# Layer 0 of a two-layer encoder: branch B first, in Strassen pairs, then attention; part of the conditioning and of the slice sums on GpSimd

## Chip, core and metric

One core of one Trainium2 chip runs the whole program. The metric is device time in microseconds (us) of one execution. The profile calls the engines PE (TensorE), PEld (its weight loads), DVE (VectorE), ACT (ScalarE), POOL (GpSimd) and SP (SyncE, which issues the transfers).

## What is computed

Two layers on a sequence of 512 positions with 2048 channels, in float32. Both are conditioned by a vector c: shift, scale and gate are `silu(c) @ w_mod + b_mod`, 48 tiles of 128 channels per layer (16 each).

```python
# layer 0
h = rms_norm(x, g) * (1 + scale) + shift
q, k, v, z_a, u_b, g_b, g_c, z_b = split(h @ w_in)      # eight times 1024 channels
y_a = dilated_mixture_attention(rope(q), rope(k), v) * silu(z_a)   # 8 heads of 128
y_b = g_b * short_conv(g_c * u_b, conv_w) * silu(z_b)
x = x + gate * (concatenate([y_a, y_b]) @ w_out)
# layer 1: a gated unit with position mixing and three projections of 2048 channels,
# its own conditioning, then x + gate * (y @ w_out) and a last rms_norm
```

## The kernel before

**Exact products.** Every float32 weight slice and activation is split into a rounded part and a remainder (`hi`, `lo`), and a product is three matmuls (`mm3`, L336 to L341). Weights come from memory in slices of 128x1024. A `Stream` (L252) loads each slice, ScalarE casts it to `hi` (L279), VectorE subtracts to get `lo` (L280), and it runs two slices ahead of TensorE (`next`, L323).

**Plain and Strassen tiles.** `fmajor` (L354) makes one tile of 128 channels by 512 positions out of two slices: 48 matmuls of 512 columns. `paired` (L426) makes two tiles out of four slices by Strassen's scheme: seven products of 24 matmuls of 256 columns, 168 in all. It needs sums of slices (`combined`, L283: four of the seven operands need one addition each, all on VectorE) and sums of activation blocks (`Blocks.block`, L372). Before the change pairs are used in both output projections and in layer 1, not in layer 0's input projection.

**Layer 0.** A first stage forms the normalised `h`, shift and scale, and the columns of three small groups (`AB_GROUPS`, L48). Then a loop over heads (from L690) does attention and branch B together: per head the plain tiles of q and k, `u_b`, then `scores` (L628), `g_c`, then `turned` (L647: transposes of the probabilities), `z_b`, `weighed` (L657: probabilities times values) and `g_b`. Halfway it makes the second half of the values (`tmajor`, L465). The list `AB_PLAN` (L54 to L57) is the order of the slices.

**Conditioning beside it.** `Later` (L500) is called once per slice. It spreads 64 conditioning tiles (16 gates of layer 0, all 48 of layer 1) over 88 slices. Each tile is two transfers of 128x1024 and two fused multiply-and-sum instructions on VectorE (L240). GpSimd has only the rotary products (L624) in this stage.

**Order.** A program builder places each engine's instructions in a fixed order; every engine, and SP's queue of transfers, works in that order. Buffers are few: two pairs `whi`/`wlo` and three `wraw` for weight slices, two `mraw` for conditioning.

Of the kernel before, what the change touches and what calls it, by code (L numbers as in the profile page):

```python
# [14 lines left out]
D = 2048  # L15
# [22 lines left out]
def wide(c0, n):  # L38
# [12 lines left out]
    [(A_Q, P), (A_K, P), (B_Z, P), (B_GB, P)],  # L51
# [27 lines left out]

SG_PLAIN = 3  # L80
# [29 lines left out]
def trunk(ctx, tc, xT, vecs, ab_wm, sg_wm, ab_wp, ab_wg, ab_wi, ab_wo, sg_wi, sg_wo, wsT, bs, rope, band, eye, out):  # L110
# [12 lines left out]

    class Pages:


        def __init__(self):
            self.g = [work.tile([P, 4, S], F32, tag="xy", bufs=4, name="xy") for _ in range(4)]
# [91 lines left out]
    cs = const.tile([P, KT], F32, name="cs")  # L220
    nc.scalar.activation(out=cs, in_=vec[:, V_C:V_C + KT], func=AF.Tanh, scale=0.5)
    nc.vector.scalar_tensor_tensor(out=cs, in0=cs, scalar=1.0, in1=vec[:, V_C:V_C + KT], op0=ALU.add, op1=ALU.mult)
    for i in range(4):
        acc = bank()
        for j in range(4):
            kt = 4 * i + j
            nc.tensor.matmul(acc[:, j * P:(j + 1) * P], lhsT=cs[:, kt:kt + 1].to_broadcast([P, P]), rhs=ident, start=True, stop=True)
        if i % 2:
            nc.vector.tensor_copy(out=cb[:, i * S:(i + 1) * S], in_=acc)
        else:  # L230
            nc.scalar.copy(out=cb[:, i * S:(i + 1) * S], in_=acc)

    wm = {"ab": (ab_wm, V_ABB), "sg": (sg_wm, V_SGB)}

    def mod_tile(pool, n, nt, bufs):
        src, b = wm[n]
        for h in range(2):
            raw = pool.tile([P, HALF], F32, tag="mraw", bufs=bufs, name="mraw")
            nc.sync.dma_start(out=raw, in_=src[nt, h])
            nc.vector.tensor_tensor_reduce(  # L240
                out=raw, in0=raw, in1=cb[:, h * HALF:(h + 1) * HALF], scale=0.5,
                scalar=v1(b + nt) if h == 0 else macc[n][:, nt:nt + 1], op0=ALU.mult, op1=ALU.add,
                accum_out=(mods if h else macc)[n][:, nt:nt + 1])

# [7 lines left out]
    class Stream:  # L252
# [3 lines left out]
        def __init__(self, src, n, pairs=()):  # L256
# [26 lines left out]
        def combined(self, i, p):  # L283
# [3 lines left out]
            def add(a, b):  # L287
                nc.vector.tensor_tensor(out=r[a], in0=r[a], in1=r[b], op=ALU.add)  # L288
                return r[a]

            if p == 0:
                r[0] = self.load(i, self.pool, "wsum", 2)
                of = r[0]
            elif p == 1:
                r[1] = self.load(i + 1, work, "wraw", 3)
                of = add(0, 1)
            elif p == 2:
                r[2] = self.load(i + 2, work, "wraw", 3)
# [3 lines left out]
            elif p == 4:  # L302
                nc.vector.scalar_tensor_tensor(out=r[1], in0=r[1], scalar=-1.0, in1=r[2], op0=ALU.mult, op1=ALU.subtract)
                of = r[1]
            elif p == 5:
                r[3] = self.load(i + 3, work, "wraw", 3)
                of = r[3]
            else:
                of = add(0, 3)
            self.count = getattr(self, "count", 0) + 1  # L310
            return self.split(of, *((self.pool, 1) if self.count % 3 == 0 else (work, 2)))

        def ahead(self, upto):
# [50 lines left out]

    class Blocks:
# [3 lines left out]
        def __init__(self, pool, act, halves):  # L369
            self.pool, self.act, self.halves, self.sums = pool, act, halves, [None, None]  # L370

        def block(self, j, raw=None):  # L372
# [31 lines left out]
            op(u, t, a22, ALU.add)  # L404
# [3 lines left out]
            if not j:  # L408
                self.fill("wfill", 32)

        def fill(self, tag, n):

            t = self.pool.tile([P, n], F32, tag=tag, bufs=1, name=tag)
            nc.gpsimd.memset(t[:, 0:1], 0.0)
# [50 lines left out]
    def tmajor(pos, act):  # L465

        accs = [bank() for _ in range(NT)]
        for i in range(8):
            hi, lo = pos.slice()
            for k in range(2):  # L470
                kt = 2 * i + k
                cs = slice(k * S, (k + 1) * S)
                for j, acc in enumerate(accs):
                    ts = slice(j * P, (j + 1) * P)
                    a = act[kt]
                    mm3(acc, (a[0][:, ts], a[1][:, ts]), (hi[:, cs], lo[:, cs]), kt == 0, kt == KT - 1)
        return accs
# [18 lines left out]
    s_abi, s_abo = Stream(ab_wi, len(AB_PLAN)), Stream(ab_wo, len(ABO_PLAN), PAIRS_OUT)  # L496
# [3 lines left out]
    class Later:  # L500


        def __init__(self, pool, tiles, slices):
            self.pool, self.tiles, self.step, self.at = pool, tiles, len(tiles) / slices, 0.0
# [8 lines left out]
        def one(self):  # L513
            n, nt = self.tiles.pop(0)
            mod_tile(self.pool, n, nt, 2)
            if n == "sg" and KT <= nt < 2 * KT:
                mod_scale(n, nt - KT)
# [74 lines left out]
    y = Pages()  # L592
    for f in range(6):
        twice_silu(gates[f], y[f])
    fetch(1, range(KT - 4, KT))
    quarter(1, 3)
    for f in range(2):
        twice_silu(sums[1][:, f], y[6 + f])
# [14 lines left out]
    nc.sync.dma_start(out=bandT[:, :896], in_=band)  # L613

    def values(accs):
        return [split_to(acc, "v", 4, pb) for acc in accs]
# [375 lines left out]
```

## Time and profile before

| | |
|---|---|
| median of 3 runs | 1703.43 us (1702.12 to 1704.23) |
| the profiled execution | 1700.17 us, span of its instructions 1698.4 us |
| PE busy | 1635.2 us, 96% |
| DVE busy | 1237.2 us, 73% |
| ACT busy | 626.0 us, 37% |
| POOL busy | 157.9 us, 9% |
| bytes moved | 276.36 MB, mean 163 GB/s |

A busy time counts an instruction from its start to its end, waiting for a shared resource included. Matmul records overlap, so the pace of matmuls is read from their starts.

### The profile page before, as it was taken

The numbers are of one execution on the slowest core, as the hardware profiler recorded it, in microseconds if no ns is written. First come the engines' busy times: TensorE is split into PE (matmuls) and PEld (weight loads), VectorE is DVE, ScalarE is ACT, GpSimd is POOL, SyncE is SP. The second block draws the span as 40 slices with busy tenths as digits, with TensorE's granted clock in tenths as the row PEclk, the third lists the DMA queues.
The fourth block names the chain that finished last, engine by engine and source line by source line (L and its number), as shares of the span: only waits on it lengthen the run. The fifth ranks groups of instructions, "written<-read, shape, count | busy, mean of one in ns | idle before, by whom it ended". The sixth has DMA issues, their size and how long they took to land.

```text
span 1698.4 us, 23314 instructions
## 1 busy us (share of the span) xinstructions
PE 1635.2 (96%) x9294; PEld 1430.9 (84%) x9294; DVE 1237.2 (73%) x1686; ACT 626.0 (37%) x894; POOL 157.9 (9%) x110
## 2 busy tenths in 40 slices
PE   5898999999999999999999999999989999999996
PEld 4677787888888888888899988888889999988995
DVE  7899649776766777766978781224988887897874
ACT  3232324232323322323644451222244444464551
POOL 2465620000000000000000000000000000000002
PEclk7999999999999999999999999999999999999998
DMA  8787544665667665664544422222123333335322
GB/s 310 246 289 281 179 133 145 225 227 203 215 212 239 210 227 191 221 214 146 173 139 141 168 100 87 95 92 99 63 100 100 100 117 118 102 119 191 100 88 100
DMA packets 86989, 276.36 MB, mean 163 GB/s; under 512 B 8800, under 2 KB 13152, under 8 KB 86880
## 3 DMA queue, kind: packets, MB, share of 16 engines
q1 hardware_dynamic: 86880, 274.87, 47.8%
q8 instruction: 73, 1.20, 0.3%
q14 instruction: 36, 0.29, 0.0%
HBM read 266.45 MB, written 8.39 MB: 162 GB/s over the span
## 4 chain that ended last, share of the span: by engine, by line
PE 82%; DVE 10%; issue 2%; DMA 2%; ACT 2%; POOL 0%; SPq 0%; DVEq 0%; ACTq 0%; POOLq 0%
PE ps L341 27%; PE ps L340 27%; PE ps L339 27%; DVE mraw L240 3%; DVE wlo L280 2%; DMA mraw<-in_ab_wm_dram 1%; PE ps L856 1%; ACT whi L279 1%; PE ps L653 1%; DMA wraw<-in_ab_wp_dram 1%; DVE lh L487 1%; DVE xy L911 1%; DVE gsc_ab L247 1%; DMA xy<-in_xT_dram 1%; DVE tmp L482 0%
## 5 line engine op out<-in xcount | busy, mean ns | idle before, releaser
L339 PE MATMUL ps<-hh,whi 128*128 128x512 f32 (+1 forms) x1800 | 630.7, 352 | 21.5 <-ACT hh L486 12.8
L341 PE MATMUL ps<-hh,wlo 128*128 128x512 f32 (+1 forms) x1800 | 633.5, 352 | 2.5 <-DVE wlo L280 1.7
L340 PE MATMUL ps<-lh,whi 128*128 128x512 f32 (+1 forms) x1800 | 633.1, 352 | 0.9 <-DVE lh L487 0.9
L279 ACT CAST whi<-wraw 128x1024 fp32r<-128x1024 f32 x229 | 240.3, 1052 | 533.2 <-PE ps L340 343.5
L280 DVE TENSOR_TENSOR wlo<-wraw,whi 128x1024 fp32r<-128x1024 f32 x229 | 279.6, 1224 | 206.7 <-ACT whi L279 201.6
L339 PEld LDWEIGHTS ps<-hh,whi 128*128 128x128 f32 x1800 | 342.7, 191 | 70.8 <-ACT hh L486 16.5
L341 PEld LDWEIGHTS ps<-hh,wlo 128*128 128x128 f32 x1800 | 343.3, 191 | 48.5 <-DVE wlo L280 2.4
L340 PEld LDWEIGHTS ps<-lh,whi 128*128 128x128 f32 x1800 | 343.7, 191 | 45.8 <-DVE lh L487 1.7
L341 PE MATMUL ps<-shi,wlo 128*128 128x256 f32 x736 | 205.5, 279 | 3.0 <-DVE wlo L280 3.0
L340 PE MATMUL ps<-slo,whi 128*128 128x256 f32 x736 | 204.8, 278 | 0.0
L339 PE MATMUL ps<-shi,whi 128*128 128x256 f32 x736 | 204.7, 278 | 0.0
L279 ACT CAST whi<-wsum 128x1024 fp32r<-128x1024 f32 x92 | 96.7, 1051 | 164.5 <-DVE wsum L288 80.5
L339 PE MATMUL ps<-whi,hh 128*128 128x512 f32 x384 | 151.0, 393 | 2.2 <-DVE xy L571 2.1
L240 DVE CUSTOM_DVE_ANT_0 mraw<-mraw,cb,vec 128x1024 f32<-128x1024 f32 x96 | 137.1, 1428 | 21.3 <-DMA mraw<-in_sg_wm_dram 18.2
L340 PE MATMUL ps<-wlo,hh 128*128 128x512 f32 x384 | 149.9, 390 | 0.1
L341 PE MATMUL ps<-whi,lh 128*128 128x512 f32 x384 | 149.7, 390 | 0.0
L341 PEld LDWEIGHTS ps<-shi,wlo 128*128 128x128 f32 x736 | 138.3, 188 | 4.6 <-DVE wlo L280 4.6
L280 DVE TENSOR_TENSOR wlo<-wsum,whi 128x1024 fp32r<-128x1024 f32 x92 | 112.4, 1222 | 36.2 <-ACT whi L279 35.8
L339 PEld LDWEIGHTS ps<-shi,whi 128*128 128x128 f32 x736 | 138.4, 188 | 0.0
L340 PEld LDWEIGHTS ps<-slo,whi 128*128 128x128 f32 x736 | 138.4, 188 | 0.0
L545 POOL TENSOR_TENSOR wlo<-wraw,whi 128x512 fp32r<-128x512 f32 (+1 forms) x64 | 116.9, 1847 | 101.0 <-ACT whi L544 89.5
L339 PEld LDWEIGHTS ps<-whi,hh 128*128 128x128 f32 x384 | 72.4, 188 | 19.4 <-DVE xy L571 4.1
(161 smaller groups left out, 1493.0 us busy)
## 6 DMA issues: line engine op xcount, KB each, us to landing
mraw<-in_ab_wm_dram SPq DMA_DIRECT2D x96, 512.0 KB, 4.6
mraw<-in_sg_wm_dram SPq DMA_DIRECT2D x96, 512.0 KB, 4.6
wraw<-in_ab_wi_dram SPq DMA_DIRECT2D x92, 512.0 KB, 3.8
wraw<-in_sg_wi_dram SPq DMA_DIRECT2D x83, 512.0 KB, 3.5
wraw<-in_ab_wo_dram SPq DMA_DIRECT2D x27, 512.0 KB, 3.5
wraw<-in_sg_wo_dram SPq DMA_DIRECT2D x27, 512.0 KB, 3.9
wraw<-in_ab_wg_dram SPq DMA_DIRECT2D x48, 256.0 KB, 3.0
wsum<-in_sg_wi_dram SPq DMA_DIRECT2D x13, 512.0 KB, 4.2
```

The lines of the kernel that those rows point to most:

```text
L240: nc.vector.tensor_tensor_reduce(out=raw, in0=raw, in1=cb[:, h * HALF:(h + 1) * HALF], scale=0.5, scalar=v1(b + nt) if h == 0 else macc[n] ...
L247: nc.vector.scalar_tensor_tensor(out=gsc[n][:, kt:kt + 1], in0=mods[n][:, KT + kt:KT + kt + 1], scalar=1.0, in1=g, op0=ALU.add, op1=ALU.mult)
L279: nc.scalar.copy(out=hi, in_=raw)
L280: nc.vector.tensor_tensor(out=lo, in0=raw, in1=hi.bitcast(F32), op=ALU.subtract)
L339: nc.tensor.matmul(acc, lhsT=w[0], rhs=m[0], start=first, stop=False, **kw)
L340: nc.tensor.matmul(acc, lhsT=w[0], rhs=m[1], start=False, stop=False, **kw)
L341: nc.tensor.matmul(acc, lhsT=w[1], rhs=m[0], start=False, stop=last, **kw)
L487: nc.vector.scalar_tensor_tensor(out=lo[:, cols], in0=xr[:, cols], scalar=sh, in1=hi[:, cols].bitcast(F32), op0=ALU.add, op1=ALU.subtract)
L545: nc.gpsimd.tensor_tensor(out=lo, in0=raw, in1=hi.bitcast(F32), op=ALU.subtract)
L653: nc.tensor.transpose(out=pt[:, i * P:(i + 1) * P], in_=ps[i][:, ks], identity=ident)
L856: nc.tensor.matmul(acc[:, j * P:(j + 1) * P], lhsT=vt[j][f // 4][:, (f % 4) * P:(f % 4 + 1) * P], rhs=wst[:, gs], start=True, stop=True)
L911: (nc.gpsimd if f in pool else nc.vector).tensor_tensor(out=t, in0=t, in1=r, op=ALU.mult)
```

## The change

All of branch B comes before attention. The second tile of `u_b` and `g_c` takes the place of the first q and k in the small groups; then come the second half of the values (`tmajor`), six pairs (`u_b`, `g_c`) and seven pairs (`g_b`, `z_b`). Attention follows alone, with 16 plain tiles of q and k. The gate path z_a and the values wait in memory meanwhile. In the pairs two of the four sums of slices go to GpSimd (`adder`). 32 conditioning tiles of layer 1 are multiplied on GpSimd and summed on ScalarE (`mod_tile_beside`); 16 tiles of layer 0 stay on VectorE, during attention; the last 16 of layer 1 go to layer 1, with a second copy of silu(c) spread by 16 matmuls. Layer 0's output projection begins with the B half of the slices of its first four tiles (`early`). The diff, cut to its core:

```diff
-for _h in range(1, 8):
-    if _h == 4:
-        AB_PLAN += wide(A_V + 512, 512)
-    for _c in (A_Q, A_K, B_U, B_GC, B_Z, B_GB):
-        AB_PLAN += rows(_c + _h * P)
+AB_PLAN += wide(A_V + 512, 512)
+for _h in range(1, 8):
+    if _h > 1:
+        AB_PLAN += pair(order(HALVES_AB), B_U + _h * P, B_GC + _h * P)
+    AB_PLAN += pair(order(HALVES_AB), B_GB + _h * P, B_Z + _h * P)
+PAIRS_AB = range(8, len(AB_PLAN))
+for _h in range(8):
+    for _c in (A_Q, A_K):
+        AB_PLAN += rows(_c + _h * P)
...
+    def mod_tile_beside(pool, n, nt, bufs):
+        for h in range(2):
+            raw = pool.tile([P, HALF], F32, tag="mraw", bufs=bufs, name="mraw")
+            nc.sync.dma_start(out=raw, in_=wm[n][0][nt, h])
+            nc.gpsimd.tensor_tensor(out=raw, in0=raw, in1=cb[:, h * HALF:(h + 1) * HALF], op=ALU.mult)
+            nc.scalar.activation(out=raw, in_=raw, func=AF.Identity, scale=0.5, accum_out=(mods if h else macc)[n][:, nt:nt + 1])
...
             elif p == 4:
-                nc.vector.scalar_tensor_tensor(out=r[1], in0=r[1], scalar=-1.0, in1=r[2], op0=ALU.mult, op1=ALU.subtract)
-                of = r[1]
+                of = add(1, 2, self.adder)
...
             else:
-                of = add(0, 3)
+                of = add(0, 3, self.adder)
...
+    s_abi.adder = nc.gpsimd
+    later = Later(pb, [("sg", nt) for nt in range(22)], 99, mod_tile_beside)
...
+    for j, acc in enumerate(tmajor(pos, h, lambda i: i in (1, 3) and blocks.block(i // 2))):
...
+    for hd in range(1, HEADS):
+        if hd > 1:
+            u, g = page("tmp", 4), page("tmp", 4)
+            x = paired(pos, blocks, u, g)
...
+        g, z = page("tmp", 4), page("tmp", 4)
+        x = paired(pos, blocks, g, z)
...
+    beside = Later(pb, rest + [("sg", nt) for nt in range(22, 2 * KT)], 30, mod_tile_beside)
+    later = Later(pb, [("ab", nt) for nt in range(2 * KT, 3 * KT)], 30)
...
+    q = rotated(fmajor(pos, h))
...
+    k = rotated(fmajor(pos, h))
+    for hd in range(HEADS):
+        ps = scores(q, k)
+        if hd + 1 < HEADS:
+            q = rotated(fmajor(pos, h))
+        pts = turned(ps)
...
+        if hd + 1 < HEADS:
             k = rotated(fmajor(pos, h))
...
         weighed(hd, pts, v)
...
+        steps = [(f, h) for h in (1, 0) for f in range(OUT_PLAIN)] if early else [(f, h) for f in range(OUT_PLAIN) for h in range(2)]
...
+    cb2 = pc.tile([P, D], F32, tag="cb2", bufs=1, name="cb2")
+    spread_cb(cb2)
+    last = Later(pc, [("sg", nt) for nt in range(2 * KT, 3 * KT)], 20, lambda pool, n, nt, bufs: mod_tile(pool, n, nt, bufs, cb2))
```

Two places show how the order of the instructions moves. The first is POOL between the first stage and the end of layer 0. Before, the products of the first stage (L545) are followed by the rotary products (L624):

```order
L545 TENSOR_TENSOR wlo<-wraw,whi 128x768
L545 TENSOR_TENSOR wlo<-wraw,whi 128x512
L545 TENSOR_TENSOR wlo<-wraw,whi 128x768
L545 TENSOR_TENSOR wlo<-wraw,whi 128x512 x12
L624 TENSOR_TENSOR tmp<-tmp,ropeT 128x512 x16
```

Now conditioning products (`mraw<-mraw,cb`) and sums of slices (L328) stand there; this is the stretch from the values to the third pair, and the pattern goes on through all 13:

```order
L263 TENSOR_TENSOR mraw<-mraw,cb 128x1024 x5
L328 TENSOR_TENSOR wraw<-wraw 128x1024
L263 TENSOR_TENSOR mraw<-mraw,cb 128x1024
L328 TENSOR_TENSOR xy<-xy,wraw 128x1024
L263 TENSOR_TENSOR mraw<-mraw,cb 128x1024 x2
L328 TENSOR_TENSOR wraw<-wraw 128x1024
L328 TENSOR_TENSOR xy<-xy,wraw 128x1024
L263 TENSOR_TENSOR mraw<-mraw,cb 128x1024 x3
```

In the 13 pairs GpSimd now has 66 instructions of 128x1024, 40 products and 26 sums, where it had none.

The second place is ACT around the last head's scores: the copies of `rotated`, the cast of the rotated key (`hqk`), the exponentials (`p,den`) and the casts of the transposed probabilities (`hpt`). Before:

```order
L620 COPY tmp<-ps 64x512
L621 COPY tmp<-ps 64x512
L332 CAST hqk<-tmp 128x512
L279 CAST whi<-wraw 128x1024 x2
L696 COPY u<-ps 128x512
L641 ACTIVATE p,den<-p,mx 128x512 x4
L279 CAST whi<-wraw 128x1024 x2
L332 CAST hpt<-ps 128x512 x2
```

Now:

```order
L730 COPY tmp<-ps 64x512
L798 CAST hh<-xy 128x512 x4
L370 CAST hqk<-tmp 128x512
L798 CAST hh<-xy 128x512
L750 ACTIVATE p,den<-p,mx 128x512 x4
L370 CAST hpt<-ps 128x512 x4
```

The tile of `u_b` whose copy (L696) stood between the key's cast and the exponentials is gone, and so are the two weight slices (L279) of the tile between the exponentials and the transposes; in the other heads one tile is still between these two.

## Rows read from the trace of the kernel before

**Rows 1.** The page: span and busy times of the engines.
```profile
span 1698.4 us, 23314 instructions
...
PE 1635.2 (96%) x9294; PEld 1430.9 (84%) x9294; DVE 1237.2 (73%) x1686; ACT 626.0 (37%) x894; POOL 157.9 (9%) x110
```

**Rows 2.** Timeline of PE in a head of layer 0: start, duration, line, operation.
```profile
650.08 0.39 PE L339 MATMUL ps<-hh,whi 128*128 128x512 f32 x1
...
659.60 0.39 PE L339 MATMUL ps<-hh,whi 128*128 128x512 f32 x1
```

**Rows 3.** Timeline of PE in layer 1: second product of two pairs.
```profile
1275.58 0.28 PE L339 MATMUL ps<-shi,whi 128*128 128x256 f32 x1
...
1472.13 0.29 PE L339 MATMUL ps<-shi,whi 128*128 128x256 f32 x1
```

**Rows 4.** Busy time by stretch: heads of layer 0, pairs of layer 1, first stage.
```profile
core 0: us, PE busy (x) PEld busy (x) DVE busy (x) ACT busy (x) POOL busy (x), PEclk, DMA share, GB/s
640.00:722.00 82.00, 82.00 (x380) 68.08 (x378) 59.06 (x102) 25.50 (x38) 2.58 (x2) 1.00 0.60 206
1275.00:1472.00 197.00, 197.00 (x1686) 197.00 (x1685) 159.67 (x172) 92.92 (x130) 0.00 (x0) 1.00 0.34 108
85.00:127.00 42.00, 39.52 (x163) 30.94 (x162) 38.52 (x44) 16.22 (x27) 28.52 (x16) 0.96 0.85 291
```

**Rows 5.** Groups by line and shape, DVE and ACT: busy us, mean ns.
```profile
L280 DVE TENSOR_TENSOR wlo<-wraw,whi 128x1024 fp32r<-128x1024 f32 x229 | 279.6, 1224 | 206.7 <-ACT whi L279 201.6 <-PE ps L856 4.2
L446 DVE TENSOR_TENSOR tmp<-ps,tmp 128x256 f32<-128x256 f32 x23 | 9.8, 424 | 14.0 <-PE ps L341 14.0
L493 DVE SCALAR_TENSOR_TENSOR tmp<-tmp 128x512 f32<-128x512 f32 x13 | 8.9, 684 | 0.0
L668 DVE SCALAR_TENSOR_TENSOR xy<-u,vec,xy 128x511 f32<-128x511 f32 x7 | 5.2, 748 | 0.1
L279 ACT CAST whi<-wraw 128x1024 fp32r<-128x1024 f32 x229 | 240.3, 1052 | 533.2 <-PE ps L340 343.5 <-PE ps L341 123.1 <-issue 50.3
L637 DVE CUSTOM_DVE_ANT_0 p<-ps,bandT 128x512 f32<-128x512 f32 x32 | 21.3, 683 | 5.7 <-PE ps L341 5.7
L643 DVE TENSOR_SCALAR p<-p,den 128x512 f32<-128x512 f32 x32 | 15.4, 484 | 0.2
```

**Rows 6.** Timeline of POOL, late first stage, while DVE has little to do.
```profile
201.00 1.84 POOL L545 TENSOR_TENSOR wlo<-wraw,whi 128x768 fp32r<-128x768 f32 x1 [2.82 <-ACT whi L544]
...
205.94 2.54 POOL L545 TENSOR_TENSOR wlo<-wraw,whi 128x512 fp32r<-128x512 f32 x2
```

**Rows 7.** Timeline, DVE and POOL side by side, first stage and first head.
```profile
138.64 2.31 DVE L240 CUSTOM_DVE_ANT_0 mraw<-mraw,cb,vec 128x1024 f32<-128x1024 f32 x1
...
139.82 2.26 POOL L545 TENSOR_TENSOR wlo<-wraw,whi 128x512 fp32r<-128x512 f32 x1
...
287.16 1.29 POOL L624 TENSOR_TENSOR tmp<-tmp,ropeT 128x512 f32<-128x512 f32 x1 [14.95 <-ACT tmp L621]
...
287.78 1.75 DVE L280 TENSOR_TENSOR wlo<-wraw,whi 128x1024 fp32r<-128x1024 f32 x1
```

**Rows 8.** Timeline of one key's rotation, from its accumulator to the cast.
```profile
696.92 0.58 ACT L620 COPY tmp<-ps 64x512 f32<-64x512 f32 x1
...
698.18 1.29 POOL L624 TENSOR_TENSOR tmp<-tmp,ropeT 128x512 f32<-128x512 f32 x1 [9.63 <-DVE wlo L280]
...
700.48 0.68 DVE L625 TENSOR_TENSOR tmp<-tmp 128x512 f32<-128x512 f32 x1
...
701.20 0.62 ACT L332 CAST hqk<-tmp 128x512 fp32r<-128x512 f32 x1 [3.10 <-DVE tmp L625]
```

**Rows 9.** Busy time by stretch around a wait of PE in layer 1.
```profile
1245.00:1248.00 3.00, 0.79 (x4) 0.33 (x2) 2.21 (x4) 1.53 (x2) 0.00 (x0) 0.99 0.50 175
1248.00:1251.00 3.00, 1.42 (x5) 1.12 (x6) 2.88 (x3) 1.04 (x1) 0.00 (x0) 0.50 0.31 109
```

**Rows 10.** The chain that ended last: the 128-column float32 matmuls of layer 1's mixing.
```profile
1187.96 14.29 PE ps L856 x128
```

More of the change, by code (lines that the diff above doesn't have):

```diff
@@ L217, in square, with spread_cb, mod_tile @@
         return sq
[L220 to L231, printed above, removed]
+    silu = const.tile([P, KT], F32, name="cs")
+    nc.scalar.activation(out=silu, in_=vec[:, V_C:V_C + KT], func=AF.Tanh, scale=0.5)
+    nc.vector.scalar_tensor_tensor(out=silu, in0=silu, scalar=1.0, in1=vec[:, V_C:V_C + KT], op0=ALU.add, op1=ALU.mult)
+    def spread_cb(cb):
+        for i in range(4):
+            acc = bank()
+            for j in range(4):
+                kt = 4 * i + j
+                nc.tensor.matmul(acc[:, j * P:(j + 1) * P], lhsT=silu[:, kt:kt + 1].to_broadcast([P, P]), rhs=ident, start=True, stop=True)
+            if i % 2:
+                nc.vector.tensor_copy(out=cb[:, i * S:(i + 1) * S], in_=acc)
+            else:
+                nc.scalar.copy(out=cb[:, i * S:(i + 1) * S], in_=acc)
+    spread_cb(cb)
     wm = {"ab": (ab_wm, V_ABB), "sg": (sg_wm, V_SGB)}
-    def mod_tile(pool, n, nt, bufs):
+    def mod_tile(pool, n, nt, bufs, cb=cb):
         src, b = wm[n]
@@ L407, in block @@
             self.sums[j] = [s1, s2, s3, split(t)]
[L408 to L414, printed above, removed]
         def operand(self, c, k):
@@ L514, in one, with rest @@
             n, nt = self.tiles.pop(0)
-            mod_tile(self.pool, n, nt, 2)
-            if n == "sg" and KT <= nt < 2 * KT:
-                mod_scale(n, nt - KT)
+            self.tile(self.pool, n, nt, 2)
+        def rest(self):
+            while self.tiles:
+                self.one()
     h = Parts()
@@ L597, in trunk @@
     for f in range(2):
-        twice_silu(sums[1][:, f], y[6 + f])
+        twice_silu(sums[1][:, f], ga[1][:, 2 + f])
+    for g in range(2):
+        nc.sync.dma_start(out=gate_spill[g], in_=ga[g])
+    nc.sync.dma_start(out=value_spill[0], in_=sums[0])
     uc = page("tmp", 4)
@@ L609, in trunk, with both @@
+    rest = later.tiles
+    pb.release()
+    pb = tc.alloc_tile_pool(name="pb", bufs=2, reuse_waits="tile")
+    beside = Later(pb, rest + [("sg", nt) for nt in range(22, 2 * KT)], 30, mod_tile_beside)
+    later = Later(pb, [("ab", nt) for nt in range(2 * KT, 3 * KT)], 30)
+    def both(after):
+        beside(after)
+        later(after)
+    pos.tick = both
     ropeT = pb.tile([P, 2, S], F32, tag="rope", bufs=1, name="ropeT")
@@ L613, in trunk, with values @@
     nc.sync.dma_start(out=bandT[:, :896], in_=band)
-    def values(accs):
-        return [split_to(acc, "v", 4, pb) for acc in accs]
+    y = Pages([group(), group()] + yb)
+    def values(n):
+        vs = []
+        for j in range(NT):
+            t = page("tmp", 4)
+            nc.sync.dma_start(out=t, in_=value_spill[n, :, j])
+            vs.append(split_to(t, "v", 4, pb))
+        return vs
     def rotated(acc):
@@ L791, in left0 @@
             modulated("sg", kt, x2[kt], r, h.add(), LEFT)
-    while later.tiles:
-        later.one()
+    beside.rest()
+    later.rest()
+    mod_join("sg", slice(0, 2 * KT))
+    nc.vector.scalar_tensor_tensor(
+        out=gsc["sg"], in0=mods["sg"][:, KT:2 * KT], scalar=1.0, in1=vec[:, V_SGG:V_SGG + KT], op0=ALU.add, op1=ALU.mult)
     pb.release()
     pm.release()
-    x2, r1, right = project(Pos(s_abo, s_sgi), "ab", y, xT, HALVES_AB, done0, wider0, left0, s_sgi)
+    x2, r1, right = project(Pos(s_abo, s_sgi), "ab", y, xT, HALVES_AB, done0, wider0, left0, s_sgi, True)
     pos = Pos(s_sgi, s_sgo)
@@ L861, in mix @@
             scalar=v1(V_LNG + f), in1=b.unsqueeze(1).to_broadcast([P, NT, P]), op0=ALU.mult, op1=ALU.add)
+    last.rest()
+    pos.tick = None
     y = Pages()
```

190 lines of the change are left out of this document (112 added, 78 removed).

## The prediction

> **What bounds the kernel now.** I read the page first. PE is busy for 1635.2 of 1698.4 us, DVE for 73% and POOL for 9% [rows 1]. The view by stretches says the same of the two stages that matter: in the heads of layer 0 PE is busy all 82 us of the window at a granted clock of 1.00, and in the pairs of layer 1 all 197 us [rows 4]. So TensorE's own pace sets both, and the reader should look at three things: what a tile costs TensorE in either form, whether the other engines keep up with the faster form, and where TensorE would have to wait that it does not now.
>
> The pace is in the starts of its matmuls. In a plain tile the 4th matmul starts at 650.08 and the 46th at 659.60 [rows 2]: 9.52 us for 42, so 0.2267 us each. Two plain tiles are 96 matmuls, 21.8 us. In layer 1 the same place of two pairs that are ten pairs apart is at 1275.58 and 1472.13 [rows 3], so a pair takes 19.66 us.
>
> All sums start from the profiled execution, 1700.2 us; the median of the runs, 1703.4, is 3.3 us above it, well inside the range. A measurement of this kernel can tell about 0.2% (3.4 us) from no change.
>
> **Part 1: the pairs on TensorE.** Thirteen pairs replace 26 plain tiles: 13 x (21.76 - 19.66) = **27 us less**. The values (`tmajor`) and the 16 tiles of q and k stay plain. This is the gain if everything else keeps pace.
>
> **Part 2: whether VectorE and GpSimd keep pace.** A pair now has on VectorE seven subtractions and two sums of 128x1024 at 1.22 us [rows 5]: 11.0 us. Three recombinations at 0.42 add 1.3 us. The branch's own work adds about 2.5 us: two taps of the convolution at 0.75 and the rest like the 0.68 us and 0.42 us rows [rows 5]. Together 14.7 us, of 19.66. (Layer 1's pairs show 159.67 us of 197 with four sums each [rows 4], 16 us a pair, and TensorE does not wait.)
>
> GpSimd gets 66 instructions of 128x1024 in the 13 pairs, 5.1 a pair. Undisturbed, 768 columns take 1.84 us and 512 take 2.54 / 2 = 1.27 [rows 6]; another 256 cost 0.57, so I estimate 2.41 us for 1024 and 12.3 us a pair. Each engine alone would fit. The rows say that they don't run beside each other. At 138.64 VectorE begins a fused multiply of two SBUF operands, takes 2.31 us and ends at 140.95; GpSimd's next one, begun at 139.82, takes 2.26 us instead of 1.27 and so has its own 1.27 us only from 140.81 on [rows 7]. Likewise the subtraction of a weight slice (L280), 1.22 us on the mean [rows 5], takes 1.75 us when it begins 0.67 us before GpSimd's rotary product ends: 0.53 us late [rows 7]. In the first stage's window VectorE and GpSimd are busy 38.52 and 28.52 of 42 us [rows 4], much of it such waiting.
>
> So in a pair two queues share one resource. VectorE's part is what has both operands in SBUF: 11.0 us and about half of the branch's work, 12.3 us. GpSimd's is 12.3 us. When they take turns, each turn saves about 0.2 us against the sum of the two alone (2.26 against 1.27 + 1.22 [rows 5 to 7]), 1.0 us a pair for 5.1 turns, and VectorE's instructions behind one another save a few hundredths, together 0.6. That packs into **23.0 us a pair**, 3.3 more than TensorE needs. It cannot pack perfectly: ScalarE's cast (1.05 us [rows 5]) stands between GpSimd's sum and VectorE's subtraction of the same slice, and ScalarE's queue has the summing of a conditioning tile, which waits for GpSimd's product, ahead of later casts. I take one such cast a pair: **24 us**, and 13 x (24.0 - 19.66) = **56 us more**. Bounds: nothing, if it all overlaps (19.66 us), and 27.0 us a pair, if GpSimd's time comes whole on top of VectorE's (14.7 + 12.3), 95 us. I stay near the packed value because that is what the turns in rows 7 show.
>
> The Trainium skill has a rule for this (SBUF — State Buffer, section Who interferes with whom): a VectorE instruction with two SBUF inputs and a GpSimd instruction that reads SBUF lock each other out for the whole instruction. By that rule the packed 23.0 us is a floor and the stage cannot gain; without it the stage would run at 19.66. The trace agrees with the rule (2.26 us for 1.27).
>
> **Part 3: attention alone.** Before, another tile lies between the end of the key's tile and the scores. Now only the 12 matmuls of the last head's weighted sum do, 12 x 0.2267 = 2.7 us; the casts of the order's second place show it. The rotation runs over four instructions: from the first copy at 696.92 to the end of the cast at 701.82 it takes 4.9 us, of which 1.0 is VectorE's queue (L625 begins at 700.48, GpSimd had ended at 699.47) [rows 8]. So 3.9 to 4.9 us against a cover of 2.7: 1.8 us of waiting in each of seven heads, 12.6. The first head has no cover, 4.5. The last head has no tile between scores and transposes: four maxima, scalings and small ones of 0.68 + 0.48 + 0.4 us [rows 5], 6.2 us on VectorE, begin about 1.4 us after the scores do, whose matmuls take 2.7; with the last exponential about 5 us are bare, and 1.5 more for the first cast and remainder of the transposed ones. `early` covers only what comes after. That is 23.6 us. GpSimd's rotary product can find a conditioning product ahead of it: half of 2.41 us a head on the mean, 8.4. And a wait can cost clock: after TensorE's wait in 1245 to 1251 the granted clock is 0.50, the lower of its two levels (1.2 of 2.4 GHz) [rows 9]; I put 5 us on that. **37 us more**; bounds 15 (rotations at their shortest, nothing for queue and clock) and 60 (every head 3 us later).
>
> **Part 4: the small ones.** The second spread of silu(c) is 16 float32 matmuls of 128 columns; 128 records of such halves take 14.29 us [rows 10], so 16 x 2 x 0.11 = 3.6 us, all on TensorE: **4 us more**. Layer 1's 16 conditioning tiles and the 16 of layer 0 on VectorE cost nothing where they are: layer 0's heads have VectorE busy 59 of 82 us with more such tiles per us [rows 4], and the cover for layer 1's is the stretch of its values, with few other VectorE instructions. Without cover a tile would cost its two instructions, some 2.5 us by the 1.22 us of the same size [rows 5]. The 8 MB of spilled gates and values move on SP's queue beside everything else: nothing. The block sums before the first pair are 26 instructions of 1.22 us [rows 5] under 43.5 us of values: I put **1 us** on that, with bounds 0 and 8.
>
> **Sum.** -27 + 56 + 37 + 4 + 1 = +71: 1700.2 + 71 = **1771 us**.
>
> **Rivals.**
> *The shared resource is no bound, and it gets faster.* If VectorE's subtractions and GpSimd's instructions overlapped, 14.7 and 12.3 us would both fit in 19.66, part 2 is nothing, attention costs its least: -27 + 0 + 15 + 4 + 1 = -7, **1693 us**. The decisive point is a pair that needs less than 19.66 us of turns. For it: each engine alone fits, and layer 1's pairs run without a wait. Against it: every meeting in rows 7. Chance 0.13.
> *Packed turns and covered heads.* Pairs at 23.0 (+43), attention at 18 by mostly short rotations: -27 + 43 + 18 + 4 + 1 = +39, **1739 us**. For it: queues have two slices of lead. Chance 0.27, with what lies around it from 1706 to 1750.
> *The queues chain up.* Conditioning loads that wait for GpSimd's buffers stand in SP's queue ahead of weight slices, and ScalarE's sums ahead of casts, so nothing packs: 27.0 us a pair (+95) and 48 in attention: -27 + 95 + 48 + 4 + 1 = +121, **1821 us**. It decides once GpSimd is more than two conditioning tiles behind. Chance 0.15, half of it above 1826.
>
> **How the numbers follow.** The forecast has 0.43, the rivals 0.13, 0.27 and 0.15; 0.02 is left for no change. The range leaves out the faster case and the upper part of the last: 1706 to 1826. Faster 0.13, within 0.2% 0.02, slower 0.85.
>
> **What would show it.** In the new profile: pairs of layer 0 at about 24 us instead of 19.66, with L320 and L328 on VectorE above 1.5 us on the mean and POOL's products above 3 us; POOL busy around 70% or more of the stage; TensorE waiting in the pairs for `wlo` or `third`; about 29 + 4 us a head with waits for `hqk`; one wait of 5 us or more at the last head's transposes. Pairs at 20 us with POOL's instructions near 2.4 would prove part 2 wrong, heads at 29 us part 3.

## The result, and the profile after

The changed kernel takes 1872.95 us (median of 4 runs, 1870.12 to 1877.19), the kernel before 1702.78: a ratio of **1.100**, interval 1.098 to 1.103. The forecast was 1771, range 1706 to 1826. It is slower, as forecast, but by 170 us and not 71, and outside the range.

The page of the profiled execution (1870.12 us), span and busy times; the lines of before are [rows 1]:

```profile
span 1868.4 us, 25750 instructions
...
PE 1672.3 (90%) x10262; PEld 1493.5 (80%) x10262; DVE 1382.3 (74%) x1690; ACT 756.2 (40%) x1107; POOL 399.5 (21%) x198
```

TensorE was busy 96% of the time and is busy 90%. No other engine comes near its limit on the mean, so the stages have to be read. First the pace of the pairs: the second product of the first and of the thirteenth pair on PE's timeline (start, duration), the place that [rows 3] showed for layer 1.

```profile
320.33 0.39 PE L377 MATMUL ps<-shi,whi 128*128 128x256 f32 x1 [1.58 <-ACT whi L319]
...
657.13 0.29 PE L377 MATMUL ps<-shi,whi 128*128 128x256 f32 x1
```

336.80 us for twelve pairs: **28.07 us a pair**, where TensorE alone needs 19.66 and I had forecast 24. The stretches of the pairs and of six heads, as in [rows 4] (window, its length, busy time and instructions of PE, PEld, DVE, ACT, POOL, granted clock, DMA share, GB/s):

```profile
320.00:657.00 337.00, 272.79 (x2015) 262.98 (x2016) 241.83 (x194) 139.70 (x201) 166.63 (x62) 0.89 0.37 130
711.00:938.00 227.00, 194.06 (x818) 155.35 (x819) 146.45 (x269) 99.37 (x172) 58.17 (x30) 0.90 0.49 165
```

In both TensorE is idle for 14 to 19% of the time, and the granted clock is 0.89 to 0.90 on the mean where it was 1.00. Six heads take 227 us, 37.8 each, against about 29 of matmuls.

Where the 170.0 us came from, by the starts of the same matmuls in both traces: up to the first pair of layer 0's output projection 866.53 became 1029.93, so **163.4 us lie in layer 0**. From there to the end of layer 1's mixing it is 3.1 (the second spread), to the first pair of layer 1 another 5.6, and the rest is 2.1 us shorter. By the terms of the prediction:

| term | forecast | measured | how measured |
|---|---|---|---|
| 13 pairs on TensorE | -27 | -27 | kept as forecast |
| VectorE and GpSimd don't keep pace | +56 | +109 | 13 x (28.07 - 19.66) |
| attention alone | +37 | +65 | the remainder of the 163.4 |
| before the first pair | +1 | +16 | first stage 0.9 later; then 320.33 - 258.68 instead of 43.5 + 2.7 |
| second spread | +4 | +3 | |
| layer 1's first pair, and the end | 0 | +3.5 | 5.6 - 2.1 |
| sum | +71 | +170 | |

(The first matmul of the values starts at 258.68, the same place of the kernel before is at 257.74; in the runs below, whose first stage is the same, it lies at 258.7 to 262.1, so this start alone can shift a run by some us. Of the rest, 43.5 us are the 192 matmuls of the values, 2.7 the first product of the pair.)

TensorE's longest waits in the pairs' stretch (waited for, us in all, times, longest):

```profile
PE ps L379 <- DVE wlo L320: 30.4, 18, 5.0
PE ps L379 <- DVE third L320: 17.3, 11, 4.1
```

The same groups as [rows 5] in the pairs' stretch: POOL and a selection of DVE (busy us, mean ns, then idle time before them and what ended it).

```profile
L263 POOL TENSOR_TENSOR mraw<-mraw,cb 128x1024 f32<-128x1024 f32 x37 | 101.4, 2754 | 92.1 <-DMA mraw<-in_sg_wm_dram 92.1
L328 POOL TENSOR_TENSOR xy<-xy,wraw 128x1024 f32<-128x1024 f32 x12 | 35.7, 2977 | 59.5 <-DVE wlo L320 40.5 <-DVE third L320 19.0
L320 DVE TENSOR_TENSOR wlo<-xy,whi 128x1024 fp32r<-128x1024 f32 x32 | 49.3, 1541 | 42.5 <-ACT whi L319 42.4
L328 DVE TENSOR_TENSOR xy<-xy,wraw 128x1024 f32<-128x1024 f32 x24 | 41.7, 1736 | 0.4
L320 DVE TENSOR_TENSOR third<-wraw,third 128x1024 fp32r<-128x1024 f32 x12 | 22.4, 1864 | 6.3 <-ACT third L319 6.3
L674 DVE SCALAR_TENSOR_TENSOR xy<-tmp,xy 128x256 f32<-128x256 f32 x6 | 13.1, 2189 | 0.1
L674 DVE SCALAR_TENSOR_TENSOR xy<-ps,xy 128x256 f32<-128x256 f32 x6 | 2.5, 412 | 0.0
```

The two rows of L674 are the clearest of the whole trace. They are one line of code and one shape. With both operands in SBUF (`tmp,xy`) the instruction takes 2189 ns on the mean, with one in PSUM (`ps,xy`) 412 ns. That isn't chance of timing: of the six `ps,xy` three run wholly inside a GpSimd instruction, in 410 or 411 ns; of the six `tmp,xy` five meet one and take 2444 to 2609, the sixth meets none and takes 425. The subtractions and sums of 1.22 us [rows 5] now take 1.54 to 1.86 us on the mean.

How VectorE comes to stand still is on the timeline around 500 to 517 us (selected rows):

```profile
500.56 0.90 SPq L262 DMA_DIRECT2D mraw<-in_sg_wm_dram  x2
...
506.52 4.75 POOL L263 TENSOR_TENSOR mraw<-mraw,cb 128x1024 f32<-128x1024 f32 x2 [8.59 <-DMA mraw<-in_sg_wm_dram]
...
508.95 1.06 ACT L264 ACTIVATE mraw<-mraw 128x1024 f32<-128x1024 f32 x1 [6.01 <-POOL mraw L263]
...
510.01 1.03 ACT L319 CAST whi<-xy 128x1024 fp32r<-128x1024 f32 x1
...
511.07 1.28 DVE L320 TENSOR_TENSOR wlo<-xy,whi 128x1024 fp32r<-128x1024 f32 x1 [5.85 <-ACT whi L319]
...
514.94 2.58 DVE L674 SCALAR_TENSOR_TENSOR xy<-tmp,xy 128x256 f32<-128x256 f32 x1
```

Conditioning halves are loaded late, GpSimd's product waits for them, ScalarE's sum (L264) waits for the product, and a weight cast (L319) stands behind that sum in ScalarE's queue; VectorE waits 5.85 us for the cast. TensorE has work in hand there: from 500 to 520 it waits 2.3 us in all. So two explanations stood side by side: **turns** (GpSimd's instructions and VectorE's with two SBUF operands exclude each other) and **queues** (casts behind sums behind products behind loads).

### The profile page after: what moved, and what is told of

The parts are those of the page before. It is cut to its first block, busy times and chain, and to the rows that moved or that the text cites. A ratio compares the mean times of both kernels' runs of the same rounds, so it can differ in the third digit from the quotient of the medians.

```text
span 1868.4 us, 25750 instructions
## 1 busy us (share of the span) xinstructions
PE 1672.3 (90%) x10262; PEld 1493.5 (80%) x10262; DVE 1382.3 (74%) x1690; ACT 756.2 (40%) x1107; POOL 399.5 (21%) x198
## 4 chain that ended last, share of the span: by engine, by line
PE 41%; DVE 6%; issue 2%; ACT 2%; DMA 1%; POOL 0%; DVEq 0%; ACTq 0%; POOLq 0%
PE ps L379 13%; PE ps L377 13%; PE ps L378 13%; DVE wlo L320 1%; PE ps L956 1%; DVE wsum L435 1%; ACT whi L319 1%; DVE third L320 1%; DVE xy L1014 1%; DVE slo L442 0%; DMA wsum<-in_sg_wo_dram 0%; DVE wraw L328 0%; POOL mraw L263 0%; ACT tmp L227 0%; DMA mraw<-in_sg_wm_dram 0%
## 5 line engine op out<-in xcount | busy, mean ns | idle before, releaser
L377 PE MATMUL ps<-hh,whi 128*128 128x512 f32 (+1 forms) x1424 | 483.9, 342 | 33.5 <-ACT hh L529 14.3
L379 PE MATMUL ps<-hh,wlo 128*128 128x512 f32 (+1 forms) x1424 | 483.0, 339 | 7.0 <-DVE wlo L320 6.2
L378 PE MATMUL ps<-lh,whi 128*128 128x512 f32 (+1 forms) x1424 | 482.2, 339 | 0.3 <-DVE lh L530 0.3
L377 PEld LDWEIGHTS ps<-hh,whi 128*128 128x128 f32 x1424 | 274.3, 193 | 67.9 <-ACT hh L529 18.0
L320 DVE TENSOR_TENSOR wlo<-wraw,whi 128x1024 fp32r<-128x1024 f32 x180 | 234.3, 1306 | 126.9 <-ACT whi L319 122.2
L319 ACT CAST whi<-wraw 128x1024 fp32r<-128x1024 f32 x180 | 188.8, 1051 | 299.4 <-PE ps L378 152.3
L379 PEld LDWEIGHTS ps<-hh,wlo 128*128 128x128 f32 x1424 | 273.6, 192 | 38.0 <-DVE wlo L320 8.4
L378 PEld LDWEIGHTS ps<-lh,whi 128*128 128x128 f32 x1424 | 274.2, 193 | 29.0 <-DVE lh L530 0.7
L263 POOL TENSOR_TENSOR mraw<-mraw,cb 128x1024 f32<-128x1024 f32 x64 | 170.3, 2673 | 239.5 <-DMA mraw<-in_sg_wm_dram 224.6
L264 ACT ACTIVATE mraw<-mraw 128x1024 f32<-128x1024 f32 x64 | 67.7, 1058 | 151.5 <-POOL mraw L263 151.5
L379 PE MATMUL ps<-shi,third 128*128 128x256 f32 x384 | 110.0, 286 | 16.3 <-DVE third L320 16.3
```

What stands on the lines that cost most here:

```text
L263: nc.gpsimd.tensor_tensor(out=raw, in0=raw, in1=cb[:, h * HALF:(h + 1) * HALF], op=ALU.mult)
L264: nc.scalar.activation(out=raw, in_=raw, func=AF.Identity, scale=0.5, accum_out=(mods if h else macc)[n][:, nt:nt + 1])
L319: nc.scalar.copy(out=hi, in_=raw)
L320: nc.vector.tensor_tensor(out=lo, in0=raw, in1=hi.bitcast(F32), op=ALU.subtract)
L377: nc.tensor.matmul(acc, lhsT=w[0], rhs=m[0], start=first, stop=False, **kw)
L378: nc.tensor.matmul(acc, lhsT=w[0], rhs=m[1], start=False, stop=False, **kw)
```

## The experiments

Each is the changed kernel with one edit and one profiled run. The kernel before ran beside them on the same chip at 1700.54 us (first four), 1703.88 (second four) and 1701.61 us (last four).

### The pairs: who makes them 28 us

**No conditioning in the pair stage** (`e1`):

```diff
-    later = Later(pb, [("sg", nt) for nt in range(22)], 99, mod_tile_beside)
+    later = Later(pb, [("sg", nt) for nt in range(22)], 99, lambda pool, n, nt, bufs: None)
```

> Leaves out the conditioning tiles of the pair stage (loads, GpSimd products, ScalarE sums); GpSimd keeps the two weight sums of a pair, 2 x 2.4 = 4.8 us. Turns theory (GpSimd and VectorE share a resource): 12.3 us of VectorE with two SBUF operands and 4.8 of GpSimd make 17.1, below TensorE's 19.66, so 20 to 21 us a pair instead of 28.07, about 1770 us. Queue theory (weight casts stand in ScalarE's queue behind conditioning sums that wait for GpSimd's product and its load): those sums are gone, 20 to 21 us a pair too. Half the tiles' time would stay if the wait were in the weight sums on GpSimd themselves: 24 us a pair, 1817 us.

**Weight sums back on VectorE** (`e2`):

```diff
-    s_abi.adder = nc.gpsimd
```

> The two weight sums of a pair go from GpSimd to VectorE; conditioning stays. VectorE then has 14.7 + 2 x 1.22 = 17.1 us a pair, GpSimd 40 products in 13 pairs, 7.4 us a pair. Turns theory: 14.7 + 7.4 = 22.1 packed, 23 to 24 us a pair, about 1810 us. Queue theory: ScalarE's sums still wait for products and loads, so 26 to 27 us a pair, about 1850 us.

**Both edits** (`e3`), the two diffs above together:

> Both: no conditioning tile in the pair stage, weight sums on VectorE, so that GpSimd has nothing to do there. Both theories: VectorE has 17.1 us a pair below TensorE's 19.66, as in layer 1, so 19.7 to 20.5 us a pair, about 1765 us. More than 22 us a pair would show a third cause (loads, spills or the branch's own chain).

**ScalarE's sums left out** (`e4`):

```diff
             nc.gpsimd.tensor_tensor(out=raw, in0=raw, in1=cb[:, h * HALF:(h + 1) * HALF], op=ALU.mult)
-            nc.scalar.activation(out=raw, in_=raw, func=AF.Identity, scale=0.5, accum_out=...)
```

> Only ScalarE's sums of the products are left out in the pair stage; loads and GpSimd's products stay, so GpSimd and VectorE have the same work as before the edit. Turns theory: 27 to 28 us a pair, about 1862 us. Queue theory: weight casts no longer stand behind a sum that waits, so 23 to 24 us a pair (the packed turns), about 1811 us.

Measured, with the time of a pair from the same two matmuls as above. VectorE's own work is 16.3 us a pair with the sums (196.07 us in the 239 us window of `e3`, below), 13.9 without; GpSimd's is counted at 2.41 us an instruction, the estimate of before; in the heads of the changed kernel the same products take 2.44 on the mean.

| kernel | VectorE + GpSimd, own us a pair | a pair | whole kernel |
|---|---|---|---|
| changed kernel | 13.9 + 12.3 = 26.2 | 28.07 | 1870.12 |
| `e4`, no ScalarE sums | 13.9 + 12.3 = 26.2 | 26.73 | 1866.18 |
| `e2`, sums on VectorE | 16.3 + 7.4 = 23.7 | 25.57 | 1845.32 |
| `e1`, no conditioning | 13.9 + 4.8 = 18.7 | 20.99 | 1777.06 |
| `e3`, both | 16.3 + 0 | 19.92 | 1759.55 |

The window of `e3`:

```profile
312.00:551.00 239.00, 236.59 (x2017) 235.28 (x2017) 196.07 (x221) 100.47 (x127) 0.00 (x0) 1.00 0.34 104
```

With GpSimd empty, TensorE sets the pace again: 19.92 us, clock 1.00. So part 1 of the prediction holds, and 8.15 of the 8.41 us a pair hang on GpSimd's work and what goes with it (loads, ScalarE's sums). `e1` fits both theories, as expected. `e2`, 25.57, falls between them: 23 to 24 by turns, 26 to 27 by queues. `e4` decides against the queue theory as the main cause: with the casts freed from the sums a pair still takes 26.73 us. TensorE's waits in its pairs (waited for, us, times, longest):

```profile
PE ps L388 <- DVE wlo L329: 40.0, 12, 6.8
PE ps L388 <- DVE third L329: 12.7, 6, 6.9
```

It waits for VectorE's remainders as before. So ScalarE's sums are worth 1.3 us of the 8.4: a little below the 27 to 28 that the turns theory expected, and far from the 23 to 24 of the queue theory. (The whole kernel gains only 4 us: its first pair comes 3.2 us later, mostly by the first stage, and attention takes 7.8 longer, for which no cause was looked for.)

**Fills in place of products** (`e5`). A stricter cut between the two theories: the same queue, loads, buffer and dependences, but GpSimd reads nothing.

```diff
-            nc.gpsimd.tensor_tensor(out=raw, in0=raw, in1=cb[:, h * HALF:(h + 1) * HALF], op=ALU.mult)
+            nc.gpsimd.memset(raw, 0.0)
+            nc.gpsimd.memset(raw, 0.0)
```

> Weight sums on VectorE as in the run of that edit (25.57 us a pair); in the pair stage GpSimd's product is replaced by two fills of the same buffer, which read nothing; loads, the wait of the fill for the load, ScalarE's sum behind it and all queues stay (the conditioning values are not computed). Shared-read theory (only instructions that read take turns): VectorE's subtractions return to 1.22 us, 20 to 21 us a pair, about 1768 us. Queue and latency theory: the chain load, GpSimd, ScalarE's sum, cast is still there, 24 to 25.5 us a pair, about 1835 us.

1779.98 us, **21.48 us a pair** against 25.57 with products (`e2`). The groups in its pairs, POOL and DVE:

```profile
L272 POOL MEMSET mraw<- 128x1024 f32 x36 | 34.7, 963 | 2.1
L271 POOL MEMSET mraw<- 128x1024 f32 x36 | 34.4, 955 | 185.0 <-DMA mraw<-in_sg_wm_dram 183.7 <-ACT mraw L273 1.2
...
L337 DVE TENSOR_TENSOR xy<-xy,wraw 128x1024 f32<-128x1024 f32 x37 | 45.2, 1220 | 0.5
L329 DVE TENSOR_TENSOR wlo<-xy,whi 128x1024 fp32r<-128x1024 f32 x33 | 40.4, 1224 | 22.3 <-ACT whi L328 22.2
L682 DVE SCALAR_TENSOR_TENSOR xy<-tmp,xy 128x256 f32<-128x256 f32 x6 | 2.5, 418 | 0.0
```

And in `e2`, with products, the same subtraction and a smaller sum (0.68 us in `e5`):

```profile
L320 DVE TENSOR_TENSOR wlo<-xy,whi 128x1024 fp32r<-128x1024 f32 x33 | 48.5, 1471 | 25.4 <-ACT whi L319 25.4
L671 DVE TENSOR_TENSOR xy<-tmp,xy 128x512 f32<-128x512 f32 x6 | 13.3, 2223 | 0.0
```

Under fills VectorE's instructions take their own time, though GpSimd is filling during 4.2 us of VectorE's work in each pair. Two fills take 1.92 us where a product takes 2.41, so the load on GpSimd's queue is a little lighter; but that VectorE is not touched at all shows that it is the reading that excludes. Of the 5.65 us that conditioning costs a pair here (25.57 - 19.92), 4.1 go with the reading and 1.6 stay with queues and loads. 21.48 lies half a us above the range of the shared-read theory and far below the other's.

**One more slice of lead** (`e6`):

```diff
-            self.ahead(i + 2)
+            self.ahead(i + 3 if i in self.deep else i + 2)
...
+    s_abi.deep = range(8, 97)
```

> Weight slices of the pairs are prepared one slice earlier in program order (three slices in the three buffers that exist), GpSimd's work unchanged. Latency theory (turns make the chain sum, cast, subtraction longer than the lead, and packed turns would take 23 us): 24 to 25 us a pair, about 1825 us. Sum theory (GpSimd's 12.3 us and VectorE's 14.7 us add whatever the lead, as 27.0, 24.5 and 19.5 did in three runs): 27 to 28 us a pair, about 1865 us.

1869.49 us and 27.43 us a pair: the lead is worth 0.6 us. So the extra over my packed 23.0 is not a matter of latency that one more slice of lead would hide.

What it is shows when the starts and ends of all VectorE and GpSimd instructions between the two matmuls above are laid over each other. Per pair of the changed kernel VectorE is in an instruction for 20.16 us, GpSimd for 13.87, both at once for 9.36 (one of them waiting, mostly), hence at least one of them for 24.68 and **neither for 3.39**. In `e6` neither runs for 2.87, in `e4` for 2.39. I had 23.0 and 1.0 for these two. Which steps make up the 3.39 is only half settled: ScalarE is busy in 1.88 of them, mostly with the cast between a sum and its subtraction.

### The heads

**The query one head further ahead** (`a1`):

```diff
     k = rotated(fmajor(pos, h))
+    q = [q, rotated(fmajor(pos, h))]
     for hd in range(HEADS):
-        ps = scores(q, k)
+        ps = scores(q.pop(0), k)
         if hd + 1 < HEADS:
-            q = rotated(fmajor(pos, h))
+            k = rotated(fmajor(pos, h))
         pts = turned(ps)
...
-        if hd + 1 < HEADS:
-            k = rotated(fmajor(pos, h))
+        if hd + 2 < HEADS:
+            q.append(rotated(fmajor(pos, h)))
```

(and three buffers for the rotated tiles instead of two)

> Attention alone: the query's tile is computed one head further ahead, so that in every head but the last two a whole tile (11 us) lies between the end of the key's tile and the scores; nothing else changes. Rotation theory (heads take 37.4 us on the mean because the key's rotation is uncovered, and the wait costs clock behind it): waits for the rotated key vanish, 29 to 31 us a head up to the sixth, about 1870 - 45 = 1825 us. GpSimd theory (heads are long since GpSimd's conditioning products take turns with VectorE and stand ahead of the rotary product): still 34 to 36 us a head, about 1855 us.

**No conditioning by GpSimd in the heads** (`a2`):

```diff
-    beside = Later(pb, rest + [("sg", nt) for nt in range(22, 2 * KT)], 30, mod_tile_beside)
+    beside = Later(pb, rest + [("sg", nt) for nt in range(22, 2 * KT)], 30, lambda pool, n, nt, bufs: None)
```

> Leaves out the conditioning tiles that go by GpSimd in the heads (loads, products, sums); the order of the tiles stays. Rotation theory: a rotation still takes at least 3.9 us against 2.7 us of cover, and the wait still costs clock: 34 to 36 us a head, about 1850 us. GpSimd theory: 29 to 31 us a head, about 1820 us.

**Both** (`a3`), the last two diffs together:

> Both edits: query one head further ahead and no conditioning tile by GpSimd in the heads. Either theory: 29 to 30 us a head, about 1815 us; more than 32 us a head would be a third cause (the probabilities' chain on VectorE and ScalarE).

| kernel | a head (mean of the first six) | last pair to the output projection | whole kernel |
|---|---|---|---|
| changed kernel | 37.8 | 372.8 | 1870.12 |
| `a1`, query ahead | 33.9 | 345.9 | 1843.73 |
| `a2`, no GpSimd conditioning | 35.4 | 358.5 | 1855.42 |
| `a3`, both | 29.1 | 312.1 | 1809.94 |

Neither theory had it alone: 27 and 14 us singly, 61 together. TensorE's waits in six heads say why. The changed kernel:

```profile
PE ps L377 <- ACT hqk L370: 24.1, 5, 8.5
PE ps L377 <- ACT hpt L370: 9.1, 2, 4.9
PE ps L378 <- DVE lpt L371: 6.6, 5, 2.6
PE ps L378 <- DVE lqk L371: 1.3, 1, 1.3
```

`a1`:

```profile
PE ps L377 <- ACT hpt L370: 9.4, 3, 5.1
PE ps L378 <- DVE lpt L371: 5.7, 2, 3.7
PE ps L762 <- DVE p L752: 3.9, 4, 1.7
```

`a2`:

```profile
PE ps L379 <- ACT hqk L372: 21.8, 7, 6.8
PE ps L380 <- DVE lpt L373: 5.3, 6, 0.9
```

`a3`:

```profile
PE ps L764 <- DVE p L754: 0.9, 1, 0.9
```

The wait for the rotated key (`hqk`) is the missing cover: it goes in `a1` and stays in `a2`. What is left in `a1`, the probabilities and their casts (`p`, `hpt`, `lpt`), is the conditioning beside them: it goes in `a3`. How that conditioning delays them was not tested by itself. The longest of these waits in `a1` is the queue, not a turn: a GpSimd product waits 8.33 us for its load, ScalarE's sum 6.10 for the product, and the cast of the probabilities stands behind two such sums and two copies of the next rotation:

```profile
844.57 2.39 POOL L263 TENSOR_TENSOR mraw<-mraw,cb 128x1024 f32<-128x1024 f32 x1 [8.33 <-DMA mraw<-in_sg_wm_dram]
...
846.99 1.06 ACT L264 ACTIVATE mraw<-mraw 128x1024 f32<-128x1024 f32 x1 [6.10 <-POOL mraw L263]
...
849.57 1.06 ACT L264 ACTIVATE mraw<-mraw 128x1024 f32<-128x1024 f32 x1 [1.43 <-POOL mraw L263]
...
851.93 1.07 ACT L370 CAST hpt<-ps 128x512 fp32r<-128x512 f32 x2
...
852.57 0.79 PE L377 MATMUL ps<-hpt,hv 128*128 128x512 f32 x1 [5.12 <-ACT hpt L370]
```

The windows of the six heads of `a2`, and then of `a3`:

```profile
708.00:920.00 212.00, 191.44 (x816) 153.07 (x816) 134.98 (x266) 79.44 (x136) 15.50 (x12) 0.93 0.38 132
```

```profile
713.00:888.00 175.00, 174.14 (x814) 143.86 (x812) 130.51 (x264) 81.69 (x136) 16.75 (x12) 1.00 0.44 156
```

The same matmuls: of the 37 us between them 19.7 are idle time of TensorE (20.6 against 0.9) and 17.3 are longer matmul time. About 13 of these 17.3 are the clock: in `a2` 26 us of matmul time lie at the lower clock level, twice what they would need; in `a3` there are none. The other 4 were not traced. A wait here costs nearly twice its length.

### Layer 1's first pair

The load of the first slice, its cast and TensorE's wait, on the timeline of the changed kernel (before, the wait in this place is the one in [rows 9], 3.3 us):

```profile
1412.88 3.87 SPq L310 DMA_DIRECT2D wsum<-in_sg_wi_dram  x2
...
1420.04 1.04 ACT L319 CAST whi<-wsum 128x1024 fp32r<-128x1024 f32 x1 [5.02 <-DMA wsum<-in_sg_wi_dram]
...
1421.13 0.58 PE L377 MATMUL ps<-hh,whi 128*128 128x256 f32 x1 [8.80 <-ACT whi L319]
```

The edit (`c1`) takes the turn of the other half of the room:

```diff
         unit(f, [(accs[0], ALL)], accs[1], page("tmp", 4))
+        if f == 1:
+            s_sgi.raws()
```

> Layer 1 alone: the first load of a first product goes into the other half of the room that the block sums used, whose last reader is two VectorE instructions earlier. If the wait of 8.8 us before the first pair of layer 1 is that load waiting for the room: the wait falls by 2 to 5 us, 1866 us. If it is VectorE's block sums themselves that are late: nothing, 1870 us.

1867.92 us. The stretch from the projection's first pair to layer 1's is 393.7 us instead of 397.2, 3.5 less, and the wait is 5.2 us instead of 8.8. So 3.6 us of it are the load that waits for the room: stream and block sums now share two halves, and the first slice got the half that was read last. The rest, 1.9 us more than before, stays open.

### What the order is worth, and a complete version

**The order without GpSimd** (`e7`), the diffs of `a1`, `a2` and `e3` together:

> The new order without GpSimd: weight sums on VectorE, no conditioning tile in the pair stage, none by GpSimd in the heads (32 tiles of layer 1's conditioning are left out of layer 0), query one head further ahead. The bare order: pairs 19.9 us, heads 29.2 us, about 1699 us (1810 less 13 x 8.1 and 6 before the first pair). If the parts don't add up, 1720 us or more.

**All conditioning on VectorE** (`b1`), the diffs of `a1`, `e2` and `c1`, and:

```diff
-    later = Later(pb, [("sg", nt) for nt in range(22)], 99, mod_tile_beside)
+    later = Later(pb, [("sg", nt) for nt in range(12)], 99)
...
-    beside = Later(pb, rest + [("sg", nt) for nt in range(22, 2 * KT)], 30, mod_tile_beside)
+    beside = Later(pb, rest + [("sg", nt) for nt in range(12, 2 * KT)], 30)
...
-    mod_join("sg", slice(0, 2 * KT))
```

> A complete kernel: the new order with all conditioning on VectorE (12 tiles over the pairs, 36 over the heads, 2.44 us each), weight sums on VectorE, query one head further ahead, the other half of the room in layer 1. VectorE then has 17.1 + 2.3 = 19.4 us a pair and about 20 + 11 us a head, both at TensorE's 19.7 and 29. If VectorE can be filled to the brim: 1700 to 1705 us. If a queue at its limit makes TensorE wait and lose clock: 22 us a pair and 33 us a head, about 1755 us.

`e7` takes 1698.69 us, 2.9 less than the kernel before beside it, 0.17%, which a measurement can't tell from no change. And it leaves out 32 of the 64 conditioning tiles. Layer 0's output projection begins at 858.1 instead of 866.5; layer 1's spread and first pair cost 9 again. Those 8.4 us are what is left of 23.3 in the pairs (13 x (21.76 - 19.97)): the first stage ends 2.9 later in this run, the stretch before the first pair takes 4.8 more than its matmuls need, and the remainder, about 7, is attention. So the bare order has nothing to give to pay for those tiles.

`b1` takes 1740.93 us, 129 less than the changed kernel and 39 more than the kernel before. Its windows of the pairs and of the heads:

```profile
312.00:568.00 256.00, 245.16 (x2019) 241.16 (x2018) 216.51 (x261) 100.97 (x127) 0.00 (x0) 0.98 0.40 138
618.00:846.00 228.00, 207.52 (x929) 166.04 (x927) 204.22 (x399) 101.60 (x180) 22.08 (x15) 0.98 0.66 215
```

VectorE is busy for 85 and 90%, a pair takes 21.31 us and a head 32.4: between the two expectations. With VectorE filled that far TensorE waits, in the pairs 10.8 us: 6.7 behind ScalarE's copies of the accumulators (`tmp`) and 4.1 for VectorE's remainders. That VectorE's full queue holds up the copies too is likely, but not shown. No version found here beats the kernel before.

## Why the prediction was right and wrong

**Part 1, TensorE's pace: right.** 19.92 us (`e3`) and 19.97 us (`e7`) a pair against 19.66.

**Part 2, turns: the mechanism was right, the size wrong.** The step that failed is "That packs into 23.0 us a pair" with "one such cast a pair". In its terms: of 14.7 + 12.3 = 27.0 us I let 4.0 overlap (2.4 of VectorE's work without two SBUF operands, 1.0 for turns, 0.6 for VectorE back to back), which left 23.0, and added 1.0 for a cast. Measured: of 26.2 us only 1.5 overlap, which leaves 24.7, and for 3.4 neither engine works. That is 53 of the 99 us by which the sum fell short. The upper bound, 27.0 ("if GpSimd's time comes whole on top of VectorE's"), was exceeded too, because it had no idle time at all. A better rule for this kernel is in the table of the pairs: the two own times added, plus some 2 us (26.2, 23.7 and 18.7 became 28.07, 25.57 and 20.99), and TensorE's pace where that is longer. It is fitted to these three runs, and the 2 us depend on the queues: without ScalarE's sums 26.2 became 26.73 (`e4`). My figure for VectorE, 14.7 us, was 0.8 too high, which hid a part of the error.

The Trainium skill (SBUF — State Buffer, section Who interferes with whom) says that a GpSimd instruction that only writes does not contend with a VectorE instruction with two SBUF inputs, and that a VectorE instruction with at most one SBUF input doesn't contend with GpSimd at all, outside VectorE's two-port modes. The runs agree with both: 1.22 us under fills, 412 ns for `ps,xy` where `tmp,xy` takes 2189.

**Part 3, attention: three steps mis-sized.** 65 us against 37, above the upper bound of 60. "1.8 us of waiting in each of seven heads" was 3.1 even with GpSimd free (21.8 us in seven waits, `a2`) and 4.8 with it (24.1 in five). "5" for the clock was the worst: in `a2` against `a3` it is about 13 us in six heads. And conditioning was charged only to the rotary product's place in GpSimd's queue, not to the probabilities' chain on ScalarE and VectorE, where `a1` still waits 19 us. The last head, 6.5 us in the forecast, shows one wait of 2.35 before the transposes and 0.33 behind: overestimated.

**Part 4: the spread was right, the block sums not.** I put 1 us on the stretch before the first pair, with 8 as the bound. From the first matmul of the values to the first pair's second product the changed kernel takes 61.6 us, where the matmuls need 46.2: 15 lost. With GpSimd empty it takes 51.4 (`e3`), with fills 52.4 (`e5`), with products alone 62.3 (`e2`). So 10 of the 15 are the same turns, of GpSimd's first products with VectorE's block sums and their remainders (`slo`, 1771 ns on the mean there, 1222 with GpSimd empty). The other 5 stay with GpSimd empty, and what they are was not tested. That layer 1's first slice would wait for the shared room was not in the prediction at all: it names no reader of that room.

**The rivals.** "The queues chain up" came nearest in time (1821), with 27.0 us a pair. Its mechanism was not the main one in the pairs: without ScalarE's sums a pair is 1.3 us shorter and the kernel 4, and with loads and all queues in place but fills for products (`e5`) a pair takes 21.48. In the heads queues did play a part. "The shared resource is no bound" and "packed turns and covered heads" fell.

**What would show it.** L320 and L328 above 1.5 us, TensorE's waits for `wlo` and `third`, and waits for `hqk` in the heads came as named, though a head took 37.8 us and not 33. GpSimd's products above 3 us (2.75) and POOL busy for 70% of the stage (49%) did not: GpSimd waits 92 us of 337 for its loads and most of 79 for what its sums read, and still the turns set most of the loss: VectorE's subtractions and sums take 1.54 to 1.86 us instead of 1.22.

## What to carry to other kernels

Before work is moved to GpSimd, count VectorE's instructions that read two SBUF operands in that stage: where most of them do, as here, both engines' own times add, and in this kernel up to 2 us on 26 came on top, so the sum has to stay well under TensorE's time. An engine that looks 50% free is no room. When an order is changed, look at each producer chain (rotation, softmax) for the TensorE work that lay over it: uncovered, it costs its wait and, in these heads, two thirds as much again at the lower clock. And where two users come to share a buffer room, ask which half the next load gets and who read it last.

## What the runs showed that was not expected

GpSimd's fills beside VectorE cost VectorE nothing (1220 and 1224 ns, as alone), while products of the same shape in the same places cost it 0.22 us on the mean of its 128x1024 instructions (1.44 in `e2`, 1.22 in `e5`). Small instructions are hit hardest: a 128x256 update of 0.42 us took 2.19. And the clock's share of a wait: about 13 us of slower matmuls for 19.7 us of idle time in six heads.
